# Decoder layer on one core: second norm's variance scaling and normalisation moved to VectorE, ada dots two places earlier

## The chip, the cores and the metric

The kernel runs on one core of a Trainium2 chip. The metric is the device time of one execution in microseconds (us), as a median of several runs.

## The reference

One layer of a decoder trunk, 256 tokens (two halves of 128), model width 1024, float32.

```python
mod = silu(c) @ w_ada + b_ada                      # 6 x 1024: shift, scale, gate, twice
h = layer_norm(x) * (1 + sc1) + sh1
rq, rk, rv, rg, mq, mk, mv = split(h @ w_in)       # 7 x 512 columns
y_ret = silu(rg) * groupnorm(retention(rq, rk, rv))
y_moba = block_causal_softmax_attention(mq, mk, mv)
x = layer_norm(alpha * x + g1 * (concat(y_ret, y_moba) @ w_out), ln1_w, ln1_b)
h = layer_norm(x) * (1 + sc2) + sh2
gate, up = split(h @ w_ffn_in)                     # 2 x 2816 columns
x = layer_norm(alpha * x + g2 * ((silu(gate) * up) @ w_ffn_out), ln2_w, ln2_b)
```

## The kernel before

**Weights.** All weights are loaded from HBM by SyncE's queue in units of 128 x 2048 float32 (1 MB). A unit is used as two parts: ScalarE casts it to a rounded "hi" part (`split_hi`, L109) and VectorE subtracts that to give a "lo" part (`split_lo`, L114), in pieces of 128 x 1024. TensorE then does three matmuls for each product (`mm3`, L123 to L125). Six load buffers are shared by a list of units (`items`, L213 to L226). `Stream.drop` frees a buffer and issues the next load of the list, so the order of the list and the places of the drops fix when each load is issued.

**The modulation.** `mod` is not computed on TensorE. Its weights come in 24 units `ada0` to `ada23`; `dot(u)` (L174) does two VectorE multiply-and-sum operations over 128 x 1024 (L166), drops the unit, and adds the bias (L170; on GpSimd from unit 8 on). Units 0 to 7 scale and shift the first projection, 8 to 11 are the first gate, 12 to 19 shift and scale the input of the feed-forward part, 20 to 23 are the second gate. The bias of column block k of the feed-forward input comes from unit 12 + k.

**Order of work.** The body from L553 to L809 has its order fixed by hand for VectorE, ScalarE, TensorE and SyncE: each engine runs its operations in the order in which the code names them. GpSimd runs in order too. The stages are:

1. First projection (`pa`, L263): eight weight units `wa0` to `wa7`, each after its `dot`. At its end the eight accumulators are copied out: rq, mq, rv by ScalarE (L596, L601, L603), rk by VectorE (L597).
2. Retention and attention (`Retention`, L278; `Moba`, L316), with the key, value and gate projections of units `wb0` to `wb5` between them. For each retention head VectorE applies the decay to the scores (L290) and takes statistics (L303 to L307), GpSimd raises the variance to -0.5 (L147), ScalarE normalises (L313). The head's output bank on TensorE comes back for the head after next once ScalarE has read it.
3. Output projection (`pw`, `out_rows`, L401) of token half 0, then of half 1.
4. Two norms for each half. `MixNorm` (L451): residual in two column halves (L461, L462), mean and square (`row_rstd`, L444), `center` (L470), `affine` (L475). `FfnInput` (L478) is the second norm: mean of the new x (L446), ScalarE's square with the sum of squares (L447), the variance scaled by 1/D plus eps on GpSimd (L448), GpSimd's power -0.5 (L449), GpSimd's product of mean and scale (L487), ScalarE's normalisation in two column halves (L492). TensorE transposes the result (L500) and ScalarE modulates it into `hf` (L505).
5. Feed-forward part. Half 0 of the first block is multiplied with unsplit float32 weights (`plain`, L525, two passes for each matmul); everything after uses the split parts (`gu`, then `acc`).

The objects `n0`, `n1` are the first norms of the two token halves, `f0`, `f1` the second norms, `rets[h]` the retention heads.

Of the kernel before, what the change touches and what calls it, by code (L numbers as in the profile page):

```python
# [12 lines left out]
AF = mybir.ActivationFunctionType  # L13
ALU = mybir.AluOpType
# [3 lines left out]
D = 1024  # L18
# [9 lines left out]
EPS = 1e-5  # L28
# [4 lines left out]
def tile_decoder_layer(ctx: ExitStack, tc: tile.TileContext, x, c, b_ada, ln_rows, ada_u, wa_u, wb_u, wo_u,  # L33
                       fi_u, fo_u, decay, dist, out):
    nc = tc.nc
# [8 lines left out]
    def bank(name, tag):  # L44
        return pp.tile([P, 512], F32, tag=tag, name=name, bufs=4 if tag == "mm" else 2)
# [17 lines left out]
    xs = [cst.tile([P, D], F32, name=f"x{t}") for t in range(2)]  # L63
# [132 lines left out]
    dst = cst.tile([P, 384], F32, name="dst")  # L196
# [7 lines left out]
    def ada_item(u, n=1):  # L204
        return f"ada{u}", ada_u[u], n

    def wb_item(i):
        return f"wb{i}", wb_u[i], 1

    def wo_item(i):  # L210
        return f"wo{i}", wo_u[(i + 2) % 4], 1

    items = []  # L213
    for kt in range(KT):
        items += [ada_item(kt, 2), (f"wa{kt}", wa_u[kt], 2)]
    items.append(wb_item(0))
    items += [lambda i=i: nc.sync.dma_start(dec[i], decay[:, 2 * i:2 * i + 2, :]) for i in range(2)]
    items += [wb_item(1), ada_item(8), wb_item(2), ada_item(9), lambda: nc.sync.dma_start(dst, dist)]
    for i in range(3, 6):
        items += [wb_item(i), ada_item(7 + i)]  # L220
    for i in range(4):
        items += [wo_item(i)] + ([ada_item(13 + i)] if i < 3 else [])
    items.append(lambda: nc.sync.dma_start(g1b, gates[0].to_broadcast([P, D])))
    items.append(lambda: rows_bcast(lnw, 0))
    fi = [(f"fi{i // 2}{i % 2}", fi_u[i], 1 + i // 3) for i in range(4)]
    items += [ada_item(16), ada_item(17), fi[0], ada_item(18), fi[1], fi[2], ada_item(19), fi[3]]  # L226

    def x_transpose(t, q):
        ps = bank("ps_t", "mm")
# [163 lines left out]
    def unit(name):  # L393
        w = parts_of(name)
        return w, stream[name]

    def lo_done(w, s):
        split_lo(w, s)
        stream.drop()
# [44 lines left out]
    def row_rstd(x, scratch, total, s5):  # L444
        nm, sq, v, r, m = (s5[:, i:i + 1] for i in range(5))
        nc.vector.tensor_scalar(total, total, -1.0 / D, 0.0, ALU.mult, ALU.add, accum_out=nm)  # L446
        nc.scalar.activation(scratch, x, AF.Square, bias=nm, accum_out=sq)  # L447
        nc.gpsimd.tensor_scalar(v, sq, 1.0 / D, EPS, ALU.mult, ALU.add)  # L448
        nc.gpsimd.tensor_tensor(r, v, mhalf[:, 0:1], ALU.pow)  # L449

    class MixNorm:  # L451
# [26 lines left out]
    class FfnInput:  # L478
# [5 lines left out]

        def variance(self):
            row_rstd(xs[self.t], self.xh, self.total, self.st)
            nc.gpsimd.tensor_tensor(self.st[:, 4:5], self.st[:, 0:1], self.st[:, 3:4], ALU.mult)  # L487

        def normalize(self):
            for q in range(2):  # L490
                cs = slice(q * 512, (q + 1) * 512)
                nc.scalar.activation(self.xh[:, cs], xs[self.t][:, cs], AF.Identity, bias=self.st[:, 4:5],  # L492
                                     scale=self.st[:, 3:4])

        def transpose(self, qs=range(2)):
            for q in qs:
# [56 lines left out]
    with order():  # L553
# [22 lines left out]
        for kt in range(1, KT):  # L576
            dot(kt)
            sw, w = stream[f"wa{kt}"], parts_of(f"wa{kt}")
# [12 lines left out]

        rets, mobas = [Retention(h) for h in range(NH)], [Moba(h) for h in range(NH)]
        w, sw = unit("wb0")
        split_hi(w, sw, (0,))
        for i in range(2):
            nc.scalar.copy(rqT[:, 2 * i:2 * i + 2, :], heads(pa[i]))  # L596
            nc.vector.tensor_copy(rkT[:, 2 * i:2 * i + 2, :], heads(pa[2 + i]))  # L597
        split_hi(w, sw, (1,))
        lo_done(w, sw)
        for i in range(2):  # L600
            nc.scalar.mul(mqT[:, 2 * i:2 * i + 2, :], heads(pa[4 + i]), SCALE)  # L601
        for i in range(2):
# [1 line left out]
        for h in range(2):  # L604
            rets[h].scores()
            rets[h].decays()
        pmk = [bank(f"pmk{i}", "mm") for i in range(2)]
        w1, sw1 = unit("wb1")
        split_hi(w1, sw1)
        proj_keys(0, w, 0)  # L610
# [12 lines left out]
        proj_keys(0, w, 2)  # L623
        rets[2].values()
        rets[1].stats()
        dot(8, (0,))
        rets[1].norm()
        proj_keys(0, w, 3)
        rets[2].stats()
        dot(8, (1,))  # L630
        proj_keys(1, w1, 0)
        rets[3].values()
        w2, sw2 = unit("wb2")
# [6 lines left out]
        rets[3].norm()  # L640
        for k in range(1, 4):
            proj_keys(1, w1, k)
        dot(9)
        w3, sw3 = unit("wb3")
        split_hi(w3, sw3, (0,))
        for i in range(2):
# [18 lines left out]
        mobas[2].bias()  # L665
        mobas[2].exp()
        mobas[3].scores()
        dot(10, (0,))
        split_hi(w4, sw4, (1,))
        proj_rows(0, w2, 3, pmv)  # L670
        mobas[3].bias()
# [1 line left out]
        for i in range(2):  # L673
            mobas[i].transpose()
            mobas[i].copy()
            proj_rows(1, w3, i, pmv)
        dot(10, (1,))
        for i in range(2, 4):
            mobas[i].transpose()
            mobas[i].copy()  # L680
# [1 line left out]
        lo_done(w4, sw4)  # L682
        for m in mobas:
            m.recip()
        dot(11)
        prg = [bank(f"prg{t}", "mm") for t in range(2)]
        for t in range(2):
            nc.scalar.copy(mv_[:, t, :], pmv[t])
        dot(12)
        w5, sw5 = unit("wb5")  # L690
        split_hi(w5, sw5)
        lo_done(w5, sw5)
# [10 lines left out]
        wo = [None] * 4  # L703
        wo[0], so0 = unit("wo0")
        split_hi(wo[0], so0)
        dot(13)
        lo_done(wo[0], so0)
        nc.scalar.preload_act_table(AF.Silu)
        pv = [y_transpose(t, 1) for t in range(2)]
# [5 lines left out]
        wo[1], so1 = unit("wo1")  # L715
        split_hi(wo[1], so1)
        lo_done(wo[1], so1)
        dot(14, (0,))
        for t in range(2):
            nc.scalar.activation(sg[:, t, :], prg[t], AF.Silu)  # L720
            nc.vector.tensor_tensor(y[t][:, 0:512], y[t][:, 0:512], sg[:, t, :], ALU.mult)
        dot(14, (1,))
        wo[2], so2 = unit("wo2")
        split_hi(wo[2], so2)
        pw0 = [bank(f"pw0{h}", "mm") for h in range(2)]
# [7 lines left out]
        wo[3], so3 = unit("wo3")  # L733
        split_hi(wo[3], so3)
        lo_done(wo[3], so3)
        dot(15, (0,))
        out_rows(pw0, 0, [(h, i) for i in range(4, 6) for h in range(2)] + [(h, i) for h in range(2) for i in (6, 7)])
        pw1 = [bank(f"pw1{h}", "mm") for h in range(2)]
        rows1 = [(h, i) for h in range(2) for i in range(KT)]
        n0, n1 = MixNorm(0, pw0), MixNorm(1, pw1)  # L740
# [5 lines left out]
        n0.variance(f0.xh)  # L746
        n0.center(0)
        n0.center(1)
        dot(15, (1,))
        n0.affine(0)  # L750
        n0.affine(1)
        f0.variance()
        out_rows(pw1, 1, rows1[:15])
        dot(16)
        dot(17)
        f0.normalize()
        f0.transpose()
        out_rows(pw1, 1, rows1[15:])
        f0.modulate(range(6))
        n1.residual(0)  # L760
        n1.residual(1)
        n1.variance(f1.xh)
        n1.center(0)
        n1.center(1)
        w00, raw00 = unit("fi00")
        split_hi(w00, raw00, (0,))
        dot(18)
        f0.part_hi(0, 4)
        split_hi(w00, raw00, (1,))
        f0.modulate(range(6, 7))  # L770
# [2 lines left out]
        f1.variance()  # L773
        w01, raw01 = unit("fi01")
        split_hi(w01, raw01, (0,))
        dot(19)
        ps00, ps10 = (bank(f"gu{i}0", "at") for i in range(2))
        raw = [raw00, raw01]
        src1 = [stream["fi10"], stream["fi11"]]
# [54 lines left out]
    for b in range(2, NBLK):  # L834
        gt = new_gt(b)
        ps = [bank(f"gu{b}{t}", "at") for t in range(2)]
        for i in range(2):
            w = split(load(fi_u[2 * b + i], f"fi{b}{i}"), f"fi{b}{i}")
# [20 lines left out]
    n0, n1 = norms  # L859
# [98 lines left out]
```

## Time and profile before

| What | Value |
|---|---|
| Median of 3 runs | 339.83 us (339.35 to 341.22) |
| Profiled execution | span 338.4 us from its first to its last instruction; its time with what lies around the span is not listed apart |
| TensorE matmul busy | 317.7 us (94%) |
| VectorE busy | 245.9 us (73%) |
| ScalarE busy | 160.1 us (47%) |
| GpSimd busy | 32.9 us (10%) |
| Loads on SyncE's queue | 84.90 MB, 65.6% of the 16 DMA engines' time |
| Mean granted TensorE clock | 0.977 of full |

A busy share is an average over the stages. The chain of waits of the profile lies on TensorE for 79% of the span, on VectorE for 7%, on GpSimd for 5% and on ScalarE for 4%. Times within the span are counted from its start.

### The profile page before, as it was taken

What the parts mean: (1) busy time and instruction counts of PE and PEld (TensorE: products, weight loads), DVE (VectorE), ACT (ScalarE), POOL (GpSimd) and SP (SyncE); (2) the same over time, 40 slices, a digit from 0 to 9 for tenths busy, and PEclk for the clock granted to TensorE, in tenths of its full rate; (3) what the DMA queues carried; (4) which work ended last, traced back from release to release, by engine and by line L of the source; (5) the groups of instructions that cost most, each with busy time, mean ns of one, the idle gap of its engine ahead of it and who ended that gap; (6) DMA issues with size and microseconds to landing.
All of it is one profiled execution on the core that took longest, in us unless ns stands there. A gap on an engine that the chain in (4) does not pass through costs nothing.

```text
span 338.4 us, 4339 instructions
## 1 busy us (share of the span) xinstructions
PE 317.7 (94%) x1612; PEld 262.9 (78%) x1612; DVE 245.9 (73%) x394; ACT 160.1 (47%) x249; POOL 32.9 (10%) x48
## 2 busy tenths in 40 slices
PE   4499999999999998899999999999999999999990
PEld 4379999998888886436788888888888888888890
DVE  2699996688999898796997666684545454547485
ACT  2455352726958711849955353535353535354000
POOL 1300000054021006260000000000000000000011
PEclk9789999999999999799999999999999999999996
DMA  7999999857599995556799767966464644000011
GB/s 228 416 410 408 409 411 423 322 200 279 221 371 387 378 402 176 212 215 247 253 428 420 302 239 258 365 236 265 136 237 138 236 134 178 0 3 1 0 62 62
DMA packets 16036, 85.18 MB, mean 252 GB/s; under 512 B 2048, under 2 KB 2704, under 8 KB 8592
## 3 DMA queue, kind: packets, MB, share of 16 engines
q1 hardware_dynamic: 15984, 84.90, 65.6%
q8 instruction: 12, 0.20, 0.2%
q14 instruction: 8, 0.07, 0.1%
q10 hardware_dynamic: 32, 0.01, 0.0%
HBM read 83.85 MB, written 1.06 MB: 251 GB/s over the span
## 4 chain that ended last, share of the span: by engine, by line
PE 79%; DVE 7%; POOL 5%; ACT 4%; DMA 2%; issue 1%; SPq 0%; DVEq 0%; POOLq 0%; ACTq 0%
PE gu L125 11%; PE gu L124 11%; PE gu L123 11%; PE pa L263 9%; PE acc L123 5%; PE acc L124 5%; PE acc L125 5%; PE pa L254 2%; DMA x<-in_x_dram 2%; ACT xh L447 1%; PE ps_gt L537 1%; PE prg L125 1%; PE prg L123 1%; PE prg L124 1%; DVE l_wo L114 1%
## 5 line engine op out<-in xcount | busy, mean ns | idle before, releaser
L114 DVE TENSOR_TENSOR l_fi<-s_fi,h_fi 128x1024 fp32r<-128x1024 f32 x44 | 52.4, 1221 | 25.6 <-ACT h_fi L109 25.6
L123 PE MATMUL gu<-h_fi,h2h 128*128 128x512 f32 x160 | 63.1, 394 | 0.0
L124 PE MATMUL gu<-l_fi,h2h 128*128 128x512 f32 x160 | 62.6, 391 | 0.0
L125 PE MATMUL gu<-h_fi,h2l 128*128 128x512 f32 x160 | 62.5, 390 | 0.0
L109 ACT CAST h_fi<-s_fi 128x1024 fp32r<-128x1024 f32 x44 | 45.1, 1057 | 30.3 <-PE gu L125 24.0
L166 DVE SCALAR_TENSOR_TENSOR junk<-s_ada,cb 128x1024 f32<-128x1024 f32 x48 | 58.6, 1222 | 0.8
L114 DVE TENSOR_TENSOR l_fo<-s_fo,h_fo 128x1024 fp32r<-128x1024 f32 x22 | 26.2, 1220 | 14.2 <-ACT h_fo L109 14.2
L125 PEld LDWEIGHTS gu<-h_fi,h2l 128*128 128x128 f32 x160 | 30.0, 188 | 6.6 <-DVE h2l L514 0.4
L123 PEld LDWEIGHTS gu<-h_fi,h2h 128*128 128x128 f32 x160 | 30.0, 188 | 6.5 <-ACT h2h L510 0.3
L124 PEld LDWEIGHTS gu<-l_fi,h2h 128*128 128x128 f32 x160 | 30.1, 188 | 6.2 <-issue 0.2
L124 PE MATMUL acc<-l_fo,gt 128*128 128x512 f32 x80 | 31.9, 399 | 0.0
L123 PE MATMUL acc<-h_fo,gt 128*128 128x512 f32 x80 | 31.7, 399 | 0.0
L109 ACT CAST h_fo<-s_fo 128x1024 fp32r<-128x1024 f32 x22 | 22.2, 1060 | 19.8 <-PE acc L125 12.2
L125 PE MATMUL acc<-h_fo,gt 128*128 128x512 f32 x80 | 31.3, 391 | 0.0
L530 ACT ACTIVATE sl<-gu 128x256 f32<-128x256 f32 x22 | 8.4, 385 | 27.4 <-PE gu L125 27.4
L531 DVE TENSOR_TENSOR sl<-sl,gu 128x256 f32<-128x256 f32 x22 | 9.1, 416 | 13.4 <-ACT sl L530 13.4
L125 PEld LDWEIGHTS acc<-h_fo,gt 128*128 128x128 f32 x80 | 15.1, 188 | 3.0
L123 PEld LDWEIGHTS acc<-h_fo,gt 128*128 128x128 f32 x80 | 15.0, 188 | 3.0
L124 PEld LDWEIGHTS acc<-l_fo,gt 128*128 128x128 f32 x80 | 15.0, 188 | 2.7
L114 DVE TENSOR_TENSOR l_wa<-s_wa,h_wa 128x1024 fp32r<-128x1024 f32 x14 | 17.1, 1219 | 0.0
L170 POOL TENSOR_TENSOR mod<-acc,bada 128x2 f32<-128x2 f32 x16 | 7.0, 438 | 101.8 <-DVE junk L166 101.8
L109 ACT CAST h_wa<-s_wa 128x1024 fp32r<-128x1024 f32 x14 | 14.4, 1041 | 4.8 <-DMA s_wa<-in_w_in_a_dram 4.7
(174 smaller groups left out, 588.1 us busy)
## 6 DMA issues: line engine op xcount, KB each, us to landing
s_fi<-in_w_ffn_in_dram SPq DMA_DIRECT2D x21, 1024.0 KB, 4.8
s_ada<-in_w_ada_dram SPq DMA_DIRECT2D x16, 1024.0 KB, 5.1
s_fo<-in_w_ffn_out_dram SPq DMA_DIRECT2D x11, 1024.0 KB, 4.8
s_ada<-in_w_ada_dram SPq DMA_DIRECT2D x16, 512.0 KB, 10.2
s_wa<-in_w_in_a_dram SPq DMA_DIRECT2D x16, 512.0 KB, 9.6
s_wb<-in_w_in_b_dram SPq DMA_DIRECT2D x6, 1024.0 KB, 10.5
s_wo<-in_w_out_dram SPq DMA_DIRECT2D x4, 1024.0 KB, 6.0
x<-in_x_dram SPq DMA_DIRECT2D x2, 512.0 KB, 6.1
```

Of the source, the lines that this page charges most:

```text
L109: nc.scalar.copy(w[0][:, cs], s[:, cs])
L114: nc.vector.tensor_tensor(w[1][:, cs], s[:, cs], w[0][:, cs].bitcast(F32), ALU.subtract)
L123: nc.tensor.matmul(o, a[0], b[0], start=first, stop=False, skip_group_check=not check)
L124: nc.tensor.matmul(o, a[0], b[1], start=False, stop=False, skip_group_check=not check)
L125: nc.tensor.matmul(o, a[1], b[0], start=False, stop=last, skip_group_check=not check)
L166: nc.vector.scalar_tensor_tensor(junk, s[:, j * D:(j + 1) * D], 1.0, cb, ALU.mult, ALU.mult, accum_out=acc[:, j:j + 1])
L170: (nc.vector if u < 8 else nc.gpsimd).tensor_tensor(mod[:, u, :], acc, bada[:, u, :], ALU.add)
L254: nc.tensor.matmul(o, sw[:, m * P:(m + 1) * P], xk, start=m % 2 == 0, stop=False, skip_group_check=True)
L263: nc.tensor.matmul(pa[m // 2][:, (m % 2) * T:(m % 2) * T + T], w[i][:, m * P:(m + 1) * P], b, start=False, stop=kt == KT - 1 and b is lk, ...
L447: nc.scalar.activation(scratch, x, AF.Square, bias=nm, accum_out=sq)
L530: nc.scalar.activation(s, ps[:, 0:256], AF.Silu)
L531: nc.vector.tensor_tensor(s, s, ps[:, 256:512], ALU.mult)
```

## The change

Three things are edited.

1. In `row_rstd`, which both norms of a half use, the scaling of the variance (L448) goes from GpSimd to VectorE, in place. In `FfnInput` the product on GpSimd (L487) is dropped and the normalisation (L492) goes from ScalarE to VectorE as one two-operand operation, (x + negated mean) * scale.
2. The list of loads has each ada unit from 8 on two places earlier among the weight units; what was `dot(u)` at a place of the code is now `dot(u + 2)` there, and the two dots left over, `dot(8)` and `dot(9)`, go to the end of the first projection.
3. The split of `wb0` is done whole, and its buffer dropped, ahead of the copies of rq and rk. In the second half of the order, `dot(18)` stands where 16 and 17 stood, `n1.residual(0)` and `dot(19)` follow `f0.normalize`, and the former places of 18 and 19 are empty.

```diff
-    items.append(wb_item(0))
+    items += [ada_item(8), wb_item(0)]
     items += [lambda i=i: nc.sync.dma_start(dec[i], ...) for i in range(2)]
-    items += [wb_item(1), ada_item(8), wb_item(2), ada_item(9), lambda: nc.sync.dma_start(dst, dist)]
+    items += [ada_item(9), wb_item(1), ada_item(10), wb_item(2), ada_item(11), lambda: nc.sync.dma_start(dst, dist)]
...
-    items += [ada_item(16), ada_item(17), fi[0], ada_item(18), fi[1], fi[2], ada_item(19), fi[3]]
+    items += [ada_item(18), fi[0], ada_item(19), fi[1], fi[2], fi[3]]
...
-        nc.gpsimd.tensor_scalar(v, sq, 1.0 / D, EPS, ALU.mult, ALU.add)
+        nc.vector.tensor_scalar(v, sq, 1.0 / D, EPS, ALU.mult, ALU.add)
...
         def variance(self):
             row_rstd(xs[self.t], self.xh, self.total, self.st)
-            nc.gpsimd.tensor_tensor(self.st[:, 4:5], self.st[:, 0:1], self.st[:, 3:4], ALU.mult)
...
-                nc.scalar.activation(self.xh[:, cs], xs[self.t][:, cs], AF.Identity, bias=self.st[:, 4:5],
-                                     scale=self.st[:, 3:4])
+                nc.vector.tensor_scalar(self.xh[:, cs], xs[self.t][:, cs], self.st[:, 0:1], self.st[:, 3:4],
+                                        ALU.add, ALU.mult)
...
         w, sw = unit("wb0")
-        split_hi(w, sw, (0,))
+        dot(8)
+        split_hi(w, sw)
+        lo_done(w, sw)
         for i in range(2):
             nc.scalar.copy(rqT[...], heads(pa[i]))
             nc.vector.tensor_copy(rkT[...], heads(pa[2 + i]))
-        split_hi(w, sw, (1,))
-        lo_done(w, sw)
...
         pmk = [bank(f"pmk{i}", "mm") for i in range(2)]
+        dot(9)
         w1, sw1 = unit("wb1")
...
         out_rows(pw1, 1, rows1[:15])
-        dot(16)
-        dot(17)
+        dot(18)
         f0.normalize()
+        n1.residual(0)
+        dot(19)
         f0.transpose()
         out_rows(pw1, 1, rows1[15:])
         f0.modulate(range(6))
-        n1.residual(0)
         n1.residual(1)
...
-        dot(18)
...
-        dot(19)
```

VectorE at the end of the first projection and the start of retention, before. `l_wa` and `l_wb` are lo parts of weight units, `junk` is a dot, `rkT` the copy of rk, `a` the decay of a head's scores:

```order
L114 TENSOR_TENSOR l_wa_632<-s_wa_453,h_wa_631 128x1024
L597 COPY rkT<-pa_220 128x512
L597 COPY rkT<-pa_221 128x512
L114 TENSOR_TENSOR l_wb_685<-s_wb_503,h_wb_684 128x1024 x2
L290 TENSOR_TENSOR a<-ps_s,dec_104 128x384 x2
L114 TENSOR_TENSOR l_wb_713<-s_wb_517,h_wb_712 128x1024
L290 TENSOR_TENSOR a<-ps_s,dec_105 128x384
L303 BN_STATS bsr<-ps_o 128x6 x2
```

The same place now:

```order
L114 TENSOR_TENSOR l_wa_631<-s_wa_453,h_wa_630 128x1024
L166 SCALAR_TENSOR_TENSOR junk,acc_685<-s_ada_503,cb 128x1024 x2
L114 TENSOR_TENSOR l_wb_684<-s_wb_515,h_wb_683 128x1024 x2
L598 COPY rkT<-pa_220 128x512
L598 COPY rkT<-pa_221 128x512
L290 TENSOR_TENSOR a<-ps_s,dec_104 128x384 x2
L166 SCALAR_TENSOR_TENSOR junk,acc_720<-s_ada_566,cb 128x1024 x2
L114 TENSOR_TENSOR l_wb_729<-s_wb_578,h_wb_728 128x1024
L290 TENSOR_TENSOR a<-ps_s,dec_105 128x384
L303 BN_STATS bsr<-ps_o 128x6 x2
```

`dot(8)` and the lo part of `wb0` now stand ahead of the copies of rk; `dot(9)` stands between the decays of heads 1 and 2, ahead of the first statistics.

VectorE in the second norms, before, from the end of `n0` (L475 is its affine step, L446 the mean for a second norm, L461 and L462 a residual half):

```order
L475 SCALAR_TENSOR_TENSOR x_83,mn_1327<-tmp_1329,s_1328,ln1b 128x512 x2
L446 TENSOR_SCALAR mn_1327,st_1336<-mn_1327 128x2
L166 SCALAR_TENSOR_TENSOR junk,acc_1409<-s_ada_1180,cb 128x1024 x2
L166 SCALAR_TENSOR_TENSOR junk,acc_1417<-s_ada_1227,cb 128x1024 x2
L461 TENSOR_TENSOR tmp_1333<-pw_1324,g1b 128x512
L462 SCALAR_TENSOR_TENSOR x_84,mn_1330<-x_84,tmp_1333 128x512
L461 TENSOR_TENSOR tmp_1333<-pw_1325,g1b 128x512
L462 SCALAR_TENSOR_TENSOR x_84,mn_1330<-x_84,tmp_1333 128x512
L446 TENSOR_SCALAR mn_1330,s_1332<-mn_1330 128x2
L470 SCALAR_TENSOR_TENSOR tmp_1333<-x_84,s_1332,ln1w 128x512 x2
L166 SCALAR_TENSOR_TENSOR junk,acc_1460<-s_ada_1275,cb 128x1024 x2
```

The same place now (L491 is the normalisation):

```order
L475 SCALAR_TENSOR_TENSOR x_83,mn_1343<-tmp_1345,s_1344,ln1b 128x512 x2
L446 TENSOR_SCALAR mn_1343,st_1352<-mn_1343 128x2
L448 TENSOR_SCALAR st_1352<-st_1352 128x1
L166 SCALAR_TENSOR_TENSOR junk,acc_1425<-s_ada_1196,cb 128x1024 x2
L491 TENSOR_SCALAR xh_1350<-x_83,st_1352 128x512 x2
L461 TENSOR_TENSOR tmp_1349<-pw_1340,g1b 128x512
L462 SCALAR_TENSOR_TENSOR x_84,mn_1346<-x_84,tmp_1349 128x512
L166 SCALAR_TENSOR_TENSOR junk,acc_1435<-s_ada_1254,cb 128x1024 x2
L461 TENSOR_TENSOR tmp_1349<-pw_1341,g1b 128x512
L462 SCALAR_TENSOR_TENSOR x_84,mn_1346<-x_84,tmp_1349 128x512
L446 TENSOR_SCALAR mn_1346,s_1348<-mn_1346 128x2
L448 TENSOR_SCALAR s_1348<-s_1348 128x1
```

The scaling L448 stands right behind each mean, one dot is gone from between mean and residual, the other stands between the two residual halves of `n1`, and the dots behind `n1`'s centre and mean (there were two) are gone.

## Rows read from the trace of the kernel before

**Rows 1.** Windows: us, busy us of PE, PEld, DVE, ACT, POOL, granted clock, DMA share, GB/s.
```profile
134.00:136.00 2.00, 0.04 (x1) 0.00 (x0) 1.97 (x5) 0.38 (x1) 1.80 (x4) 1.00 0.88 283
138.00:140.00 2.00, 2.00 (x5) 1.07 (x4) 1.19 (x2) 1.39 (x4) 0.00 (x0) 0.54 0.95 324
140.00:142.00 2.00, 2.00 (x4) 0.86 (x3) 1.93 (x7) 1.57 (x3) 0.24 (x1) 0.60 0.12 49
```

**Rows 2.** Timeline of DVE at the first projection's end: start, length, what, [idle before].
```profile
61.54 0.69 DVE L597 COPY rkT<-pa 128x512 f32<-128x512 f32 x1 [5.27 <-PE pa L263]
```

**Rows 3.** Timeline of SP's queue in the first projection.
```profile
44.99 0.33 SPq L75 DMA_DIRECT2D s_wb<-in_w_in_b_dram  x1
```

**Rows 4.** DMA issues of the page: count, KB each, median us to landing.
```profile
s_wb<-in_w_in_b_dram SPq DMA_DIRECT2D x6, 1024.0 KB, 10.5
```

**Rows 5.** Timeline of DVE in the retention stage.
```profile
65.26 1.21 DVE L290 TENSOR_TENSOR a<-ps_s,dec 128x384 f32<-128x384 f32 x2 [0.16 <-PE ps_s L286]
66.39 1.22 DVE L114 TENSOR_TENSOR l_wb<-s_wb,h_wb 128x1024 fp32r<-128x1024 f32 x1
68.67 0.56 DVE L290 TENSOR_TENSOR a<-ps_s,dec 128x384 f32<-128x384 f32 x1 [1.06 <-PE ps_s L286]
...
71.42 0.56 DVE L290 TENSOR_TENSOR a<-ps_s,dec 128x384 f32<-128x384 f32 x1 [0.18 <-PE ps_s L286]
```

**Rows 6.** Timeline of PE: head 2's values, and the first attention scores.
```profile
72.97 0.49 PE L295 MATMUL ps_o<-rv,a 128*128 128x128 f32 x2 [0.16 <-ACT y L313]
...
83.40 0.49 PE L323 MATMUL ps_ms<-mkT,mqT 128*128 128x128 f32 x2 [0.25 <-ACT mkT L647]
```

**Rows 7.** Timeline of DVE in the norms of both halves.
```profile
125.69 1.42 DVE L470 SCALAR_TENSOR_TENSOR tmp<-x,s,ln1w 128x512 f32<-128x512 f32 x2
127.02 1.22 DVE L166 SCALAR_TENSOR_TENSOR junk<-s_ada,cb 128x1024 f32<-128x1024 f32 x1
...
128.96 0.75 DVE L475 SCALAR_TENSOR_TENSOR x<-tmp,s,ln1b 128x512 f32<-128x512 f32 x1 [0.72 <-POOL s L449]
...
130.43 0.16 DVE L446 TENSOR_SCALAR_CACHE_REDUCE mn<-mn 128x2 f32<-128x2 f32 x1
...
133.04 1.22 DVE L166 SCALAR_TENSOR_TENSOR junk<-s_ada,cb 128x1024 f32<-128x1024 f32 x1
...
135.46 0.69 DVE L461 TENSOR_TENSOR tmp<-pw,g1b 128x512 f32<-128x512 f32 x1
...
138.77 0.69 DVE L461 TENSOR_TENSOR tmp<-pw,g1b 128x512 f32<-128x512 f32 x1 [1.90 <-PE pw L125]
```

**Rows 8.** Timeline of POOL in the norms.
```profile
128.37 0.56 POOL L449 TENSOR_TENSOR s<-s,mhalf 128x1 f32<-128x1 f32 x1
...
132.02 1.03 POOL L448 TENSOR_SCALAR st<-st 128x1 f32<-128x1 f32 x1 [2.93 <-ACT xh L447]
133.13 1.55 POOL L449 TENSOR_TENSOR st<-st,mhalf 128x1 f32<-128x1 f32 x1
...
148.87 1.42 POOL L449 TENSOR_TENSOR st<-st,mhalf 128x1 f32<-128x1 f32 x1
```

**Rows 9.** Timeline of ACT: the second norm's normalisation, half 0.
```profile
135.62 1.52 ACT L492 ACTIVATE xh<-x,st 128x512 f32<-128x512 f32 x2 [3.69 <-POOL st L487]
```

**Rows 10.** Timeline of DVE at the start: a normalisation of this form, 128x1024.
```profile
9.40 0.81 DVE L562 TENSOR_SCALAR xh<-x,mv_ln,r_ln 128x1024 f32<-128x1024 f32 x1
```

**Rows 11.** Timeline of PE from the second norms to the first split feed-forward matmuls.
```profile
136.48 1.36 PE L500 MATMUL ps_t<-ident,xh 128*128 128x128 f32 x8 [2.45 <-ACT xh L492]
...
138.53 12.84 PE L525 MATMUL gu<-s_fi,hf 128*128 128x512 f32 x26
151.97 0.66 PE L500 MATMUL ps_t<-ident,xh 128*128 128x128 f32 x4 [0.59 <-ACT xh L492]
...
155.07 0.80 PE L123 MATMUL gu<-h_fi,h2h 128*128 128x512 f32 x1
155.71 0.40 PE L124 MATMUL gu<-l_fi,h2h 128*128 128x512 f32 x1
```

More of the change, by code (lines that the diff above doesn't have):

```diff
@@ L215, in tile_decoder_layer @@
         items += [ada_item(kt, 2), (f"wa{kt}", wa_u[kt], 2)]
-    items.append(wb_item(0))
+    items += [ada_item(8), wb_item(0)]
     items += [lambda i=i: nc.sync.dma_start(dec[i], decay[:, 2 * i:2 * i + 2, :]) for i in range(2)]
-    items += [wb_item(1), ada_item(8), wb_item(2), ada_item(9), lambda: nc.sync.dma_start(dst, dist)]
+    items += [ada_item(9), wb_item(1), ada_item(10), wb_item(2), ada_item(11), lambda: nc.sync.dma_start(dst, dist)]
     for i in range(3, 6):
-        items += [wb_item(i), ada_item(7 + i)]
+        items += [wb_item(i), ada_item(9 + i)]
     for i in range(4):
-        items += [wo_item(i)] + ([ada_item(13 + i)] if i < 3 else [])
+        items += [wo_item(i)] + ([ada_item(15 + i)] if i < 3 else [])
     items.append(lambda: nc.sync.dma_start(g1b, gates[0].to_broadcast([P, D])))
@@ L625, in tile_decoder_layer @@
         rets[1].stats()
-        dot(8, (0,))
+        dot(10, (0,))
         rets[1].norm()
@@ L629, in tile_decoder_layer @@
         rets[2].stats()
-        dot(8, (1,))
+        dot(10, (1,))
         proj_keys(1, w1, 0)
@@ L642, in tile_decoder_layer @@
             proj_keys(1, w1, k)
-        dot(9)
+        dot(11)
         w3, sw3 = unit("wb3")
@@ L667, in tile_decoder_layer @@
         mobas[3].scores()
-        dot(10, (0,))
+        dot(12, (0,))
         split_hi(w4, sw4, (1,))
@@ L676, in tile_decoder_layer @@
             proj_rows(1, w3, i, pmv)
-        dot(10, (1,))
+        dot(12, (1,))
         for i in range(2, 4):
@@ L684, in tile_decoder_layer @@
             m.recip()
-        dot(11)
+        dot(13)
         prg = [bank(f"prg{t}", "mm") for t in range(2)]
@@ L688, in tile_decoder_layer @@
             nc.scalar.copy(mv_[:, t, :], pmv[t])
-        dot(12)
+        dot(14)
         w5, sw5 = unit("wb5")
@@ L705, in tile_decoder_layer @@
         split_hi(wo[0], so0)
-        dot(13)
+        dot(15)
         lo_done(wo[0], so0)
@@ L717, in tile_decoder_layer @@
         lo_done(wo[1], so1)
-        dot(14, (0,))
+        dot(16, (0,))
         for t in range(2):
@@ L721, in tile_decoder_layer @@
             nc.vector.tensor_tensor(y[t][:, 0:512], y[t][:, 0:512], sg[:, t, :], ALU.mult)
-        dot(14, (1,))
+        dot(16, (1,))
         wo[2], so2 = unit("wo2")
@@ L735, in tile_decoder_layer @@
         lo_done(wo[3], so3)
-        dot(15, (0,))
+        dot(17, (0,))
         out_rows(pw0, 0, [(h, i) for i in range(4, 6) for h in range(2)] + [(h, i) for h in range(2) for i in (6, 7)])
@@ L748, in tile_decoder_layer @@
         n0.center(1)
-        dot(15, (1,))
+        dot(17, (1,))
         n0.affine(0)
```

## The prediction

> **What bounds the kernel now.** I read the busy shares first: TensorE 94%, so only places where TensorE stands still or runs slowly can pay. The view by windows shows the largest: from 134 to 136 us TensorE is busy for 0.04 us, and from 138 to 142 us its granted clock is 0.54 and 0.60 on average, which is mostly the lower level, 1.2 GHz, instead of 2.4 [rows 1]. In TensorE's timeline the standstill is 2.45 us, up to 136.48, and what ends it is ScalarE's normalisation of half 0 [rows 11]; that waited 3.69 us for GpSimd [rows 9]. A second one, 0.59 us at 151.97, is half 1's normalisation; it is followed by about 0.4 us between 155.07 and 155.71, where the next step takes 0.64 us instead of some 0.23 [rows 11]. Earlier, in retention, TensorE only pauses for 0.16 us at 72.97 and 0.25 us at 83.40 [rows 6]: there the slower engines' chain and TensorE run level, with next to nothing in hand. From 160 us on TensorE does not stop until the tail, so what is gained or lost before 156 us reaches the end unchanged.
>
> **The change part by part.**
>
> *End of the first projection.* VectorE idles 5.27 us before it copies rk at 61.54, waiting for TensorE [rows 2]. `dot(8)` and the lo part of `wb0` go in there. One dot of two pieces takes 2.42 us from its start to the next operation's (133.04 to 135.46, [rows 7]), a split piece 1.22 us [rows 5], so 2.42 + 2 x 1.22 = 4.9 us: it fits, with 0.4 us left. Cost nothing; without this cover it would be 4.9 us on VectorE ahead of retention. `wb0` is now issued one place later, in the slot at 44.99 [rows 3]; with the 10.5 us of its kind [rows 4] it lands at 55.5, and its cast (2.1 us) is done before VectorE ends the dot at 58.7. SyncE's queue keeps its order, each later drop comes as early or earlier, and the decay tables behind `wb0`, needed at 65.26, have the same 10.5 us from there. ScalarE does the same casts, only sooner.
>
> *What that leaves free does not help.* VectorE now has nothing from 62.9 (61.54 + 2 x 0.69) to 65.26, when TensorE's scores arrive, because `dot(9)` stands behind the decays of heads 0 and 1.
>
> *`dot(9)` in retention.* It adds 2.42 us at 66.4, ahead of the split, the decay of head 2 and the statistics of head 0. Two waits are swallowed: 1.06 us before 68.67 and 0.18 us before 71.42 [rows 5]. So head 0's statistics come 1.4 us late and head 1's 1.2 us late. Behind head 0's stand GpSimd's power, ScalarE's normalisation and TensorE's values of head 2, which already wait at 72.97 [rows 6]: TensorE stands 1.4 us longer. Behind head 1's stand ScalarE's cast of `wb2`, the statistics of head 3, ScalarE's cast of `wb3`, the copy of the keys, and TensorE's first attention scores at 83.40, which wait too [rows 6]. With 0.25 us in hand on TensorE's own path and none on ScalarE's, those scores start 1.2 us late. Bounds: 0.3 us, if half of the dot runs in other gaps, and 2.42 us, if no wait is swallowed. I take **+1.2 us**. All later stages move by that, and I count the rest from the old times.
>
> *First norm of half 0.* The two centre operations filled VectorE's wait for ScalarE's square (125.69 to 127.02). Now L448 stands ahead of them, so VectorE waits for the square until about 127.05, then does L448 (under 0.16, the length of the small operation at 130.43), the centre (1.33) and the dot half (1.14): the affine step starts at 129.65, not at 128.96 [rows 7]. GpSimd's power is ready by then. Cost 0.7 us.
>
> *Second norm of half 0.* From affine to mean 1.47 us (128.96 to 130.43), from mean to scaling 1.59 us (130.43 to 132.02) [rows 7, 8]: 132.7. Then `dot(18)`, 2.42 us, hides GpSimd's power (0.56 to 1.55 us) [rows 8]. The normalisation starts on VectorE at 135.2; before, ScalarE started at 135.62 and took 0.76 us a half. A piece of 128x512 on VectorE lies between 0.40 us (half of the 0.81 of [rows 10]) and 0.69 us [rows 7]; I take 0.5, near the first, since that row is the same operation. TensorE restarts at **135.8 instead of 136.48**. So GpSimd's two removed operations are worth less than they look: the wait for the square, and a dot, take their place.
>
> *Half 1.* Normalisation of half 0 until 136.3, residual half (two operations of 0.69) until 137.7, `dot(19)` until 140.1, second residual half, which before started at 138.77, until 141.5. Mean to scaling 1.6: 143.1; centre 1.33, affine 1.47, mean at 145.9; scaling at 147.5; power; normalisation from 148.3, its first half done at **148.9**, where before TensorE got it at 151.97. The 1.3 us that the dot costs between the residual halves is won back from the two dots that stood behind the centre and the mean, and from L487.
>
> The power of this half took 1.42 us at 148.87 and 0.56 us at 128.37 [rows 8]. The difference is VectorE: at 128.37 it was waiting, while the power at 133.13 began just behind a dot's start at 133.04 and took 1.55. Now VectorE waits for this power, so I take 0.56. The Trainium skill (SBUF — State Buffer, "SBUF: two separate sides") says that VectorE with two SBUF inputs and GpSimd share a port pair as a lock, held for a whole instruction; by that rule too it is the short one, and without it this half would come 0.9 us later, at 149.8.
>
> *TensorE between.* 135.8 + 2.05 (136.48 to 138.53) + 12.84 (unsplit matmuls, clock fall included) = 150.7, now later than the 148.9: TensorE becomes the bound there, 1.3 us earlier than 151.97. VectorE's three split pieces (3.7) and the lo part of h (0.69) end at 153.6 or so, and TensorE reaches that point at 150.7 + 3.1 + 0.46 = 154.3, so the 0.4 us at 155.07 goes as well. **-1.7 us.**
>
> *Sum.* -1.7 + 1.2 = -0.5 us on a span of 338.4. The three runs' median, 339.83, is 1.4 above the span, which I read as what lies around it. Forecast **339.3 us**. A measurement of this kernel can tell about 0.5% (1.7 us) from no change.
>
> **The rivals.**
>
> *The clock holds.* The fall at 138 to 142 us followed the 2.45 us standstill; the 0.59 us one had none. The new standstill is 1.8 us, nearer to the first. If the clock stays at 2.4 GHz, about 1.7 us (0.46 x 2 + 0.40 x 2) [rows 1] goes off the unsplit matmuls; then VectorE's lo part at 153.6 is last, and the gain there is 2.3: 339.83 - 2.3 + 1.2 = 338.7.
>
> *`dot(9)` costs next to nothing.* VectorE's gaps and GpSimd's turn might take it, for a cost of 0.3 or less. For it: 1.24 us of waits are there; against: TensorE already waits at both places. 338.4, and with the clock held 337.8.
>
> *The clock falls in retention (slower).* TensorE's pause at 72.97 grows from 0.16 to about 1.5 us. If that is enough for the fall that followed 2.45 us, the following matmuls, which have no slack, lose the same 1.7 us: 339.3 + 1.7 = 341.0. It decides between 0.59 us (no fall) and 2.45 us (fall). Against it: no transposes or waits stand around that pause, TensorE is full before and behind.
>
> *GpSimd kept out.* The powers now start while VectorE's queue is full. If each gets in only when VectorE stops, the power of n0 ends 0.6 us behind the dot half, that of f0 0.6 us behind `dot(18)`, that of n1 0.6 us behind the centre: TensorE restarts at 137.0, the gain shrinks to 0.5, 340.5. Against it: the power at 148.87 ended at 150.29, while three split pieces ran on from 148.66.
> The Trainium skill's page SBUF — State Buffer, same section, calls the loser of that lock fully blocked; that is for one instruction, and the power at 148.87 agrees.
>
> *It doesn't do what it says.* Were `wb0` late, its split would slide behind the copies as before, at most 1 us; the 3 us in hand make this small, and I give it no chance of its own.
>
> **How the numbers follow.** Forecast 0.42, clock holds 0.23, dot for nothing 0.15, clock falls in retention 0.12, GpSimd kept out 0.08. Faster by over 0.5% (under 338.1) needs the cheap dot with or near the held clock, or the held clock and more from half 1: 0.27. Slower by over 0.5% (over 341.5) needs the fall in retention and a little more: 0.09. The rest, 0.64, is within. The range 337.6 to 341.0 takes in all five with the bounds of `dot(9)` on its cheap side, and leaves out the ends of the first and last.
>
> **What would show it.** In the changed profile: VectorE's idle before the rk copies down from 5.27 to under 1 us; a TensorE pause near 1.5 us at head 2's values; a VectorE wait on ScalarE of over 1 us at each L448; the standstill before half 0's transposes 1.8 us; none before half 1's. I am wrong if TensorE shows no new pause in retention, if the standstill of half 0 is not shorter, or if half 1 still waits for its normalisation.

## The result and the profile after

The changed kernel takes 337.72 us in the median of 5 runs (336.73 to 338.53), against 340.17 us for the kernel before (339.35 to 341.22, 5 runs): a ratio of 0.9904, 95% interval 0.9878 to 0.993. So it is faster by 1.0%, more than the 0.5% that can be told from no change. The forecast was 339.3 us, a gain too small to be told; 337.72 lies at the lower edge of its range. The profiled execution takes 336.89 us with a span of 334.9.

Part of the span's 3.5 us is not the change. The last matmul of the first projection starts at 64.18 us in the trace before and at 63.13 in the trace after, and the first transposes of the program already come 1.16 us earlier (9.10 against 10.26), ahead of anything that was changed. So I count both traces from that matmul. The last matmul of the program then comes 2.38 us earlier than before, and the medians differ by 2.45.

The windows that stood in [rows 1], from the trace after (same columns):

```profile
134.00:136.00 2.00, 0.40 (x4) 0.42 (x4) 2.00 (x5) 0.00 (x0) 0.56 (x2) 1.00 0.15 31
138.00:140.00 2.00, 2.00 (x6) 0.95 (x5) 1.97 (x5) 0.53 (x2) 0.20 (x1) 1.00 0.54 225
140.00:142.00 2.00, 2.00 (x6) 0.83 (x5) 1.12 (x5) 0.78 (x1) 0.00 (x0) 1.00 0.62 164
```

TensorE still stands for most of the time from 134 to 136 us, but the granted clock behind it is 1.00, where it was 0.54 and 0.60 [rows 1]. TensorE's timeline, against [rows 6, 11]:

```profile
73.17 0.49 PE L295 MATMUL ps_o<-rv,a 128*128 128x128 f32 x2 [1.42 <-ACT y L313]
...
133.58 0.39 PE L125 MATMUL pw<-h_wo,yl 128*128 128x512 f32 x1
135.60 1.08 PE L499 MATMUL ps_t<-ident,xh 128*128 128x128 f32 x8 [1.63 <-DVE xh L491]
...
137.21 7.89 PE L524 MATMUL gu<-s_fi,hf 128*128 128x512 f32 x18
145.28 3.70 PE L524 MATMUL gu<-s_fi,hf 128*128 128x512 f32 x8 [0.18 <-ACT hf L504]
148.81 0.60 PE L499 MATMUL ps_t<-ident,xh 128*128 128x128 f32 x4
...
150.55 1.88 PE L524 MATMUL gu<-s_fi,hf 128*128 128x512 f32 x4
151.87 0.79 PE L123 MATMUL gu<-h_fi,h2h 128*128 128x512 f32 x1
152.50 0.39 PE L124 MATMUL gu<-l_fi,h2h 128*128 128x512 f32 x1
```

The wait at head 2's values grew from 0.16 to 1.42 us. The standstill before half 0's transposes shrank from 2.45 to 1.63 us. Half 1's transposes (148.81) no longer wait; there is a new short wait for ScalarE's modulation at 145.28. VectorE's timeline, against [rows 2, 5, 7]:

```profile
60.49 1.29 DVE L598 COPY rkT<-pa 128x512 f32<-128x512 f32 x2 [0.70 <-PE pa L263]
64.21 1.21 DVE L290 TENSOR_TENSOR a<-ps_s,dec 128x384 f32<-128x384 f32 x2 [2.43 <-PE ps_s L286]
...
126.87 0.15 DVE L448 TENSOR_SCALAR s<-s 128x1 f32<-128x1 f32 x1 [1.31 <-ACT xh L447]
126.96 1.41 DVE L470 SCALAR_TENSOR_TENSOR tmp<-x,s,ln1w 128x512 f32<-128x512 f32 x2
...
132.43 0.15 DVE L448 TENSOR_SCALAR st<-st 128x1 f32<-128x1 f32 x1 [1.37 <-ACT xh L447]
132.50 1.22 DVE L166 SCALAR_TENSOR_TENSOR junk<-s_ada,cb 128x1024 f32<-128x1024 f32 x1
...
134.91 1.00 DVE L491 TENSOR_SCALAR xh<-x,st 128x512 f32<-128x512 f32 x2
...
142.50 0.15 DVE L448 TENSOR_SCALAR s<-s 128x1 f32<-128x1 f32 x1 [1.31 <-ACT xh L447]
...
146.88 0.15 DVE L448 TENSOR_SCALAR st<-st 128x1 f32<-128x1 f32 x1 [1.37 <-ACT xh L447]
```

The 5.27 us of idle time before the rk copies are down to 0.70. And VectorE now stands still four times, 1.3 to 1.4 us each, at L448: it waits there for ScalarE's square, with all its later work behind it.

### The profile page after: what moved, and what is told of

It reads as the page before. It is cut to its first block, busy times and chain, and to the rows that moved or that the text cites. A ratio compares the mean times of both kernels' runs of the same rounds, so it can differ in the third digit from the quotient of the medians.

```text
span 334.9 us, 4338 instructions
## 1 busy us (share of the span) xinstructions
PE 315.3 (94%) x1612; PEld 262.0 (78%) x1612; DVE 247.5 (74%) x402; ACT 157.5 (47%) x245; POOL 27.1 (8%) x42
## 4 chain that ended last, share of the span: by engine, by line
PE 82%; DVE 10%; ACT 3%; DMA 1%; issue 1%; POOL 1%; SPq 0%; DVEq 0%; ACTq 0%; POOLq 0%
PE gu L125 11%; PE gu L123 11%; PE gu L124 11%; PE pa L263 9%; PE acc L123 5%; PE acc L124 5%; PE acc L125 5%; DVE junk L166 3%; PE pa L254 2%; PE gu L524 2%; DMA x<-in_x_dram 1%; PE ps_gt L536 1%; ACT xh L447 1%; PE pmv L123 1%; PE pmv L125 1%
## 5 line engine op out<-in xcount | busy, mean ns | idle before, releaser
L123 PE MATMUL gu<-h_fi,h2h 128*128 128x512 f32 x160 | 63.1, 394 | 0.0
L124 PE MATMUL gu<-l_fi,h2h 128*128 128x512 f32 x160 | 62.5, 391 | 0.0
L123 PEld LDWEIGHTS gu<-h_fi,h2h 128*128 128x128 f32 x160 | 30.0, 188 | 6.4 <-ACT h2h L509 0.2
L124 PEld LDWEIGHTS gu<-l_fi,h2h 128*128 128x128 f32 x160 | 30.1, 188 | 6.2 <-DVE l_fi L114 0.2
L124 PE MATMUL acc<-l_fo,gt 128*128 128x512 f32 x80 | 31.9, 398 | 0.0
L123 PE MATMUL acc<-h_fo,gt 128*128 128x512 f32 x80 | 31.7, 398 | 0.0
L170 POOL TENSOR_TENSOR mod<-acc,bada 128x2 f32<-128x2 f32 x16 | 8.6, 535 | 164.8 <-DVE junk L166 164.8
L123 PEld LDWEIGHTS acc<-h_fo,gt 128*128 128x128 f32 x80 | 15.0, 188 | 3.0
L124 PEld LDWEIGHTS acc<-l_fo,gt 128*128 128x128 f32 x80 | 15.1, 188 | 2.6
```

What stands on the lines that cost most here:

```text
L123: nc.tensor.matmul(o, a[0], b[0], start=first, stop=False, skip_group_check=not check)
L124: nc.tensor.matmul(o, a[0], b[1], start=False, stop=False, skip_group_check=not check)
```

## The experiments

Counted from the last matmul of the first projection, the kernels agree with each other to some 0.06 us wherever their code does. So I compare four places of TensorE in that count: the first attention scores, the last matmul before the standstill, half 0's transposes behind it, and the second step of half 1's first block (L124), which stands behind TensorE's waits for the norms. From L124 to the last matmul, start to start, it is 174.5 us with the change, 174.8 before and at most 175.0 in the ten kernels. The first four columns are in us; the ratio is to the kernel before on the same chip, with its 95% interval:

| kernel | scores | last before the stop | transposes | L124 | ratio |
|---|---|---|---|---|---|
| before | 19.22 | 69.47 | 72.30 | 91.53 | 1 |
| the change | 20.20 | 70.45 | 72.47 | 89.37 | 0.9904 (0.9878 to 0.993) |
| norm edits alone | 19.20 | 69.41 | 74.01 | 93.49 | 1.0045 (1.0017 to 1.0073) |
| dots alone | 20.21 | 70.42 | 72.07 | 88.79 | 0.9918 (0.989 to 0.9946) |
| `dot(9)` early | 19.21 | 69.40 | 71.46 | 88.37 | 0.989 (0.9836 to 0.9943) |
| longer stop | 20.20 | 70.40 | 73.72 | 91.80 | 0.9983 (0.9952 to 1.0015) |
| dots, `dot(9)` early | 19.20 | 69.42 | 71.07 | 87.80 | 0.9859 (0.9826 to 0.9892) |
| residual first | 19.21 | 69.40 | 70.39 | 88.48 | 0.9882 (0.9848 to 0.9916) |
| norms in a new order | 19.21 | 69.39 | 69.63 | 86.04 | 0.9794 (0.9762 to 0.9827) |
| scaling on GpSimd | 20.19 | 70.39 | 71.14 | 88.04 | 0.9849 (0.9813 to 0.9885) |

The ratios of changed kernels up to some 2 us apart have intervals that overlap; for those the verdict rests on the count, which comes from one trace of each kernel.

After the first result my theory (A) was: the norm edits pay, but only because two dots were moved out of their way, and the clock holds because the standstill is shorter. The rivals: the norm edits alone bring the gain (B), or the dots alone do (C).

**The norm edits alone.** The kernel before with

```diff
-        nc.gpsimd.tensor_scalar(v, sq, 1.0 / D, EPS, ALU.mult, ALU.add)
+        nc.vector.tensor_scalar(v, sq, 1.0 / D, EPS, ALU.mult, ALU.add)
-            nc.gpsimd.tensor_tensor(self.st[:, 4:5], self.st[:, 0:1], self.st[:, 3:4], ALU.mult)
-                nc.scalar.activation(self.xh[:, cs], xs[self.t][:, cs], AF.Identity, bias=self.st[:, 4:5],
-                                     scale=self.st[:, 3:4])
+                nc.vector.tensor_scalar(self.xh[:, cs], xs[self.t][:, cs], self.st[:, 0:1], self.st[:, 3:4],
+                                        ALU.add, ALU.mult)
```

> The kernel before with the norm edits alone: scaling (L448) and second normalisation on VectorE, L487 gone, no dot moved. Theory A (the norm edits pay only because the dots were moved out of their way): VectorE's normalisation of half 0 now stands behind two whole dots, 4.84 us from about 132.6, so TensorE restarts near 138.1 us instead of 136.48, the standstill is about 4 us, the clock falls as before, and half 1 becomes ready at about 152.5; the time is 0.5 to 1.0 us above the kernel before: 340.7 to 341.2. Theory B (the norm edits themselves bring the gain, the dots only cost in retention): 337 us or less, since the 1.0 us in retention is not paid.

Measured: 341.92 us against 340.84 for the kernel before, slower by 0.45%, with an interval clear of 1. TensorE's timeline:

```profile
138.24 1.54 PE L499 MATMUL ps_t<-ident,xh 128*128 128x128 f32 x8 [4.21 <-DVE xh L491]
...
153.99 0.64 PE L499 MATMUL ps_t<-ident,xh 128*128 128x128 f32 x4 [1.11 <-DVE xh L491]
```

TensorE restarts at 138.24, as A had it (138.1), and the norms lose 2.0 us at L124, twice the upper end of A's 0.5 to 1.0. Half 1, which waited 0.59 us before [rows 11], waits 1.11 us. B has fallen.

**The dots alone.** The changed kernel with the three edits above undone.

> The changed kernel with the norms as before: scaling on GpSimd, normalisation on ScalarE, L487 back; all dots and splits where the change has them. Theory A: TensorE's standstill before half 0's transposes is 2.4 us or more as in the kernel before and the clock falls behind it; half 1 is ready before TensorE needs it (gain about 1.0 us), and retention costs 1.0: 340.2 us within 0.4. Theory C (the moved dots bring the gain, the norm edits little): 338 us or less.

Measured: 337.71 against 340.84. A has fallen too: the standstill did shrink without the norm edits (from 2.83 to 1.65 us, start to start), and L124 is 0.58 us earlier than with the whole change. GpSimd's timeline shows how:

```profile
133.79 1.03 POOL L448 TENSOR_SCALAR st<-st 128x1 f32<-128x1 f32 x1 [2.93 <-ACT xh L447]
134.91 0.56 POOL L449 TENSOR_TENSOR st<-st,mhalf 128x1 f32<-128x1 f32 x1
135.55 0.62 POOL L487 TENSOR_TENSOR st<-st 128x1 f32<-128x1 f32 x1
```

The power of half 0 takes 0.56 us, where it took 1.55 [rows 8]. Before, VectorE had a second whole dot beside it; now one dot ends at 134.70 and VectorE goes on with half 1's residual, which reads PSUM. So C is right in direction, and its gain is that of the moved dots together with the residual's new place, which this kernel has too; the two were not parted. I went on with a theory D: the moved dots bring the whole gain in the norms, and something in the norm edits costs.

**`dot(9)` early.** The changed kernel with

```diff
+        dot(9)
         for h in range(2):
             rets[h].scores()
             rets[h].decays()
         pmk = [bank(f"pmk{i}", "mm") for i in range(2)]
-        dot(9)
```

> The changed kernel with dot(9) put ahead of the scores of heads 0 and 1, into VectorE's 2.43 us of idle time before the first decays at 64.21. Its data was issued at 46.22 us and is there by then. Theory A (dot(9) behind the decays costs 1.0 us of TensorE's time at head 2's values and at the first attention scores): the pause at head 2's values shrinks from 1.70 to about 0.45 us, and the time falls by 1.0 us against the changed kernel: 336.7. Rival (the later stages have slack for it, the pause is made up before 160 us): within 0.3 us of the changed kernel, 337.7.

Measured: 336.34 us (before on this chip 340.84). VectorE's idle time after the rk copies takes the dot, and TensorE's wait at head 2's values is back at 0.16 us:

```profile
73.19 0.49 PE L295 MATMUL ps_o<-rv,a 128*128 128x128 f32 x2 [0.16 <-ACT y L313]
```

The scores come at 19.21, as before the change, and L124 1.00 us earlier than with the change: the whole cost of `dot(9)` is its place, and it goes through to L124 undiminished.

**A longer stop.** The changed kernel with

```diff
         dot(18)
+        dot(19, (0,))
         f0.normalize()
         n1.residual(0)
-        dot(19)
+        dot(19, (1,))
```

> The changed kernel with the first half of dot(19) (1.15 us) moved ahead of the normalisation of half 0. VectorE's work ahead of half 1 stays the same in sum. Theory A (the clock fell in the kernel before because of the 2.45 us standstill, and holds after 1.8): the standstill grows to about 3.2 us start to start, the clock falls to half for 3 to 4 us behind it, and the plain matmuls there take about 0.85 us instead of 0.43: 1.1 us from the standstill and about 1.7 from the clock, less some 0.8 of waits at 144.5 and 151.9 that they swallow: 2 us over the changed kernel, 339.7. Rival (whether the clock falls is not tied to the standstill): the clock holds, 0.3 to 0.7 us over the changed kernel, 338.2.

Measured: 340.25 us against 340.84, and L124 2.43 us later than with the change. Its windows:

```profile
136.00:138.00 2.00, 0.02 (x1) 0.05 (x1) 1.97 (x6) 0.00 (x0) 1.23 (x1) 1.00 0.36 66
138.00:140.00 2.00, 2.00 (x10) 1.87 (x11) 1.97 (x5) 1.19 (x4) 0.00 (x0) 0.59 0.99 418
140.00:142.00 2.00, 2.00 (x4) 1.12 (x4) 1.85 (x4) 1.02 (x3) 0.20 (x1) 0.55 0.23 66
```

The standstill grew to 3.32 us, start to start, and the granted clock fell behind it to 0.59 and 0.55, as before the change. Over all profiles of this study: stops of 2.83 (before), 3.32 and 4.60 us were followed by the fall to 1.2 GHz, stops of 2.06 us and less (the other seven kernels) were not. What lies between was not tried, and each kernel has one trace: whether the same stop brings the fall in every execution is not shown. This run ties the fall to the standstill. What it costs stands in TensorE's timeline:

```profile
137.98 1.58 PE L499 MATMUL ps_t<-ident,xh 128*128 128x128 f32 x8 [2.93 <-DVE xh L491]
...
140.64 11.89 PE L524 MATMUL gu<-s_fi,hf 128*128 128x512 f32 x26
```

From the transposes to the first plain matmul it is 2.66 us (1.61 with the change), and the 26 matmuls, without a wait, take 11.89 us, where they take 11.32 at 2.4 GHz in the two kernels without a wait that are shown below (dots with `dot(9)` early, norms in a new order): 1.05 + 0.57 = 1.6 us.

**Dots with `dot(9)` early.** The dots alone, with the edit of `dot(9)`.

> Dots and splits as in the change, dot(9) ahead of the scores, the norms as in the kernel before (scaling on GpSimd, normalisation on ScalarE, L487). Theory D (the moved dots bring the whole gain in the norms, the norm edits cost there): counted from the last matmul of the first projection, the second step of half 1's first block (L124) came at 91.53 us before, 89.37 with the change, 88.79 with the dots alone, 88.37 with dot(9) early; here it comes at 88.79 - 1.0 = 87.8, and the time is 0.6 us below the run with dot(9) early. Rival (the two differ by their starts alone): 88.4, no difference.

Measured: 336.17 us against 341.64 for the kernel before on that chip; L124 at 87.80, as D had it. The two pieces add up. The 0.6 us of time that D had between this run and the one with `dot(9)` early can't be told: they ran on two chips, and the intervals of their ratios overlap. TensorE's timeline, with the normalisation on ScalarE as in the kernel before and no fall of the clock:

```profile
135.00 1.36 PE L500 MATMUL ps_t<-ident,xh 128*128 128x128 f32 x8 [1.26 <-ACT xh L492]
...
136.89 11.32 PE L525 MATMUL gu<-s_fi,hf 128*128 128x512 f32 x26
```

**Half 1's residual first.** The kernel with `dot(9)` early and

```diff
-        dot(18)
-        f0.normalize()
         n1.residual(0)
+        f0.normalize()
+        dot(18)
         dot(19)
```

> The changed kernel with dot(9) early and, ahead of half 0's normalisation, half 1's first residual (1.34 us, reads PSUM) in the place of dot(18) (2.42 us, reads SBUF alone); dot(18) comes behind the normalisation. Theory E (in the changed kernel half 0 waits for dot(18), not for GpSimd's power; the power is short while VectorE reads PSUM): the power falls from 1.47 to about 0.55 us, the standstill from 2.02 to about 1.0 us start to start. VectorE reaches half 1's second residual no earlier, so half 1 becomes the bound and gives most of it back: L124 at 88.0 against 88.37, 0.3 us under the run with dot(9) early. Rival (TensorE remains the bound at half 1): the whole 1.0 us, L124 at 87.4.

Measured: 337.31 against 341.64; the stop is 0.99 us and the power 0.56, as expected, but L124 comes at 88.48, not at 88.0. TensorE's timeline shows what took it back:

```profile
134.87 1.08 PE L499 MATMUL ps_t<-ident,xh 128*128 128x128 f32 x8 [0.60 <-DVE xh L491]
...
136.49 7.89 PE L524 MATMUL gu<-s_fi,hf 128*128 128x512 f32 x18
145.74 3.70 PE L524 MATMUL gu<-s_fi,hf 128*128 128x512 f32 x8 [1.37 <-ACT hf L504]
```

I expected half 1's normalisation to be the next bound; it is ScalarE's modulation, which stands in ScalarE's order behind half 1's square and so behind both dots and the second residual. The wait of 0.18 us in the changed kernel had announced it.

**Scaling on GpSimd.** The changed kernel with L448 alone undone:

```diff
-        nc.vector.tensor_scalar(v, sq, 1.0 / D, EPS, ALU.mult, ALU.add)
+        nc.gpsimd.tensor_scalar(v, sq, 1.0 / D, EPS, ALU.mult, ALU.add)
```

> The changed kernel with L448 back on GpSimd; the normalisation stays on VectorE. Theory D: the wait for the square at the first norms is filled by the centres again and the affine step of half 0 starts 0.5 us earlier, but GpSimd's scaling takes 1.0 to 1.3 us beside VectorE's operations; half 0 is normalised right behind dot(18), 0.5 us earlier than in the changed kernel, L124 at 88.9 against 89.37. Rival (the lost time of the norm edits is the normalisation on VectorE, not the scaling): L124 stays at 89.3 or comes later.

Measured: 335.93 us against 341.64, and L124 at 88.04: 1.33 us earlier than with the change, where I expected 0.5. VectorE's timeline:

```profile
130.81 1.22 DVE L166 SCALAR_TENSOR_TENSOR junk<-s_ada,cb 128x1024 f32<-128x1024 f32 x1
...
132.07 1.23 DVE L166 SCALAR_TENSOR_TENSOR junk<-s_ada,cb 128x1024 f32<-128x1024 f32 x1
...
134.02 1.00 DVE L491 TENSOR_SCALAR xh<-x,st 128x512 f32<-128x512 f32 x2 [0.72 <-POOL st L449]
```

`dot(18)` starts right behind the mean, not behind a wait of 1.37 us, and is over before the power. The operation itself is much shorter on VectorE (0.15 us against 1.03), but there it holds up the dot behind it. So the loss inside the change is L448, and the normalisation on VectorE, without L487, is a gain: from the dots alone (88.79) to this kernel (88.04) it is 0.75 us.

**The norms in a new order.** The kernel with `dot(9)` early, and `row_rstd` cut in two, so that L448 and the power (`power()`) can be placed by themselves:

```diff
         n0.center(1)
-        dot(17, (1,))
+        n0.power()
         n0.affine(0)
         n0.affine(1)
         f0.variance()
+        dot(17, (1,))
+        f0.power()
         out_rows(pw1, 1, rows1[:15])
-        dot(18)
-        f0.normalize()
         n1.residual(0)
-        dot(19)
+        f0.normalize()
+        dot(18)
...
         n1.center(1)
+        n1.power()
...
         f1.variance()
+        dot(19, (0,))
+        f1.power()
+        dot(19, (1,))
```

> The changed kernel with dot(9) early and VectorE's order in the norms changed: the two centre operations stand ahead of L448 and fill the wait for the square, the half of dot(17) and dot(19) fill the waits for the second squares, half 1's first residual stands ahead of half 0's normalisation and dot(18) behind it. Theory E: each of the four waits of 1.31 to 1.37 us at L448 is used, half 0 is normalised at about the time of TensorE's last matmul, the standstill is at most 0.5 us start to start, half 1 comes early enough, and L124 is at 86.3 against 88.37 with dot(9) early: 2.0 us less time than that run, about 3.1 less than the changed kernel. Rival (ScalarE's order, its casts ahead of the modulation, becomes the bound): half of it, L124 at 87.3 or later.

Measured: 334.15 us (332.98 to 335.07) against 341.64, the fastest of all and 2.1% under the kernel before. TensorE's timeline (line numbers are 9 higher here):

```profile
131.96 0.40 PE L125 MATMUL pw<-h_wo,yl 128*128 128x512 f32 x1
132.20 1.04 PE L508 MATMUL ps_t<-ident,xh 128*128 128x128 f32 x8
...
133.77 11.32 PE L533 MATMUL gu<-s_fi,hf 128*128 128x512 f32 x26
144.93 0.60 PE L508 MATMUL ps_t<-ident,xh 128*128 128x128 f32 x4
...
147.98 0.79 PE L123 MATMUL gu<-h_fi,h2h 128*128 128x512 f32 x1
148.61 0.39 PE L124 MATMUL gu<-l_fi,h2h 128*128 128x512 f32 x1
```

No standstill is left: the transposes follow 0.24 us behind the last matmul. L124 is at 86.04, 2.33 us under the run with `dot(9)` early, where 2.0 was expected. This order with L448 on GpSimd was not run.

## Why the prediction was wrong

In the count from the projection's end, L124 came 2.16 us earlier, where the prediction had 0.5 (1.7 less 1.2). By its steps:

*End of the first projection: right.* One dot and the lo part of `wb0` went into the idle time at no cost; 0.70 us are left (0.4 predicted).

*`dot(9)` in retention: right.* 1.2 us predicted, 0.98 measured at the scores, and the early `dot(9)` gives all of it back. The rival of a free dot is out. So is that of a clock fall there: the wait of 1.42 us was followed by no fall.

*First norm of half 0: right.* VectorE waits 1.31 us at L448, and the affine step comes 0.5 us later (0.7 predicted). I entered 0.7 here, and the wait at the other three L448 stands in my sums as some 1.6 us from mean to scaling. What I did not do is price leaving L448 on GpSimd: with the scaling back there 1.33 us come back, more than half of the gain measured for the whole change.

*Second norm of half 0: nearly right.* In the old times TensorE restarts at 135.67, predicted 135.8. But the step "135.8 + 2.05" took the 2.05 us from the row before, in which the second half's transposes wait for ScalarE (0.72 us a piece, start to start, [rows 9]). VectorE takes 0.46, so this stretch is 1.61 us: 0.44 missed. Not all of it is the engine: with the normalisation on ScalarE and the clock held the stretch takes 1.89 us (135.00 to 136.89, dots with `dot(9)` early). So 0.28 us is VectorE's shorter piece and 0.16 is the clock, which in the old rows falls before the stretch is over (138.15 to 138.53, 0.38 us for a step that takes 0.24 with the change).

*"12.84 (unsplit matmuls, clock fall included)": this step failed.* I took the fall over because the new standstill of 1.8 us was nearer to 2.45 than to 0.59. Nearness decided nothing: the clock held. The same 26 matmuls take 11.32 us at 2.4 GHz and without a wait, so the step was 1.52 us too long; with the 0.16 from the stretch ahead the kept clock is worth 1.68, as the rival had it (1.7). That is the larger part of the error, and it is the first rival, "the clock holds", which had a chance of 0.23. The longer stop shows that the fall comes back, and costs about as much, when the standstill grows again.

*Half 1: right that it no longer binds.* Its transposes do not wait. That "the 0.4 us at 155.07 goes as well" was a misreading: it never was a wait. From L123 to L124 it is 0.63 or 0.64 us in all ten kernels, also in the norms in a new order (147.98 to 148.61). The four unsplit matmuls ahead of it take 0.43 us each (11.16 us for 26 from 133.77 to 144.93), so in the changed kernel they last from 150.55 to about 152.27, past the start of L123's row, and L124 follows 0.23 us behind. And the 0.45 us at 145.28 (start to start, over two matmuls) for ScalarE's modulation was not foreseen.

*GpSimd kept out: wrong as a rival.* The powers took 1.02, 1.47, 0.99 and 0.55 us, but the long one of half 0 ended at 134.13, before `dot(18)` did. What came later there was VectorE.

Together, on the side of more gain: 1.52 (clock), 0.44 (transposes), 0.2 (`dot(9)`), 0.13 (the restart); on the other: 0.45 (modulation) and the 0.4 at L124 that was no wait. That is 1.4 of the 1.66 us between 0.5 and 2.16; the rest is in the ends of rows that I added up as if they did not overlap. The 1.4 us that I read as what lies around the span was wrong too (340.36 us against a span of 338.0 in one execution of the kernel before, 2.4), but no term of the sum uses it. And theory A, made after the result, credited the gain to the norm edits, helped by the dots; the runs show the reverse. In parts, at L124: `dot(9)` +1.0, the other dots -3.7 (the kept clock, 1.5, among it), the normalisation on VectorE -0.75, L448 on VectorE +1.33: -2.1, against -2.16 measured. The -3.7 is the dots alone against before, 88.79 - 91.53, less the 1.0 of `dot(9)`. The parts are differences of kernels in the table, one after the other, so they close by construction; in another order they differ (the norm edits together cost 0.58 on top of the dots, 1.96 without them).

## What to carry to other kernels

An operation that waits for another engine can lose when it is moved to an engine that has other work behind it, however much shorter it is there (1.33 us here); if it is moved, put that other work ahead of it. When a standstill shrinks, price what follows at both clocks and look for a run that tells them apart, before taking one over. And when removing one wait brings less than expected, look at the small wait next to it: the 0.18 us at 145.28 had become 1.37 when half 1's residual went first.

## What the runs showed of the hardware

GpSimd's small operations depend on what VectorE is doing. The power at L449 takes 0.55 to 0.56 us beside an idle VectorE or beside the residual, which reads PSUM (134.91 with the dots alone), and 1.46 to 1.55 us behind the start of a dot; beside the centre operations it took 0.99 to 1.03. The scaling at L448 takes 0.19 us on GpSimd when VectorE is idle (145.58, scaling on GpSimd) and 1.03 to 1.28 beside a dot:

```profile
132.31 1.03 POOL L448 TENSOR_SCALAR st<-st 128x1 f32<-128x1 f32 x1 [2.92 <-ACT xh L447]
133.43 0.56 POOL L449 TENSOR_TENSOR st<-st,mhalf 128x1 f32<-128x1 f32 x1
...
145.58 0.19 POOL L448 TENSOR_SCALAR st<-st 128x1 f32<-128x1 f32 x1 [3.08 <-ACT xh L447]
145.85 0.55 POOL L449 TENSOR_TENSOR st<-st,mhalf 128x1 f32<-128x1 f32 x1
```

The Trainium skill (SBUF — State Buffer, "SBUF: two separate sides") gives the rule behind it, a port pair that is locked for a whole instruction; these rows agree. The Trainium skill also says of GpSimd "Prefer implementations on other engines where possible" (Perfetto Trace Analysis, "Optimizing GPSIMD Operations"). For L448 the runs disagree: on GpSimd it takes up to 1.1 us longer and the program is still 1.33 us shorter at L124.

The start of the program scatters more than most of these effects: the last matmul of the projection started between 62.57 and 65.00 us in the ten profiles, with nearly the same work up to there. Of these 2.43 us, 1.44 are there at the program's first transposes (9.06 to 10.50). The scatter goes into every ratio above; its cause stays open.
